# A 512-token attention and ConvFFN layer in split fp32: one plain column pair taken out and the transfers at three seams reordered

## The chip, the cores and the metric

The kernel runs on one NeuronCore of a Trainium2 chip. The metric is device time of one execution in microseconds (us), as the median of the runs shown; less is better. One profiled execution of the kernel before is read beside these runs.

## What is computed

One decoder layer over x (512 tokens, 2048 wide, float32): an attention block and then a feed-forward block, each between two RMS norms and added to its input. The change lies wholly in the second:

```python
h = rms_norm(x, norm_g[i, 2])
x = x + rms_norm(conv_ffn(h, ffn_w_up[i], ffn_conv[i], ffn_w_down[i]), norm_g[i, 3])

def conv_ffn(h, w_up, conv_w, w_down):
    u = h @ w_up                       # 2048 x 11264
    c = causal width-3 depthwise convolution of u over the tokens
    gate, val = jnp.split(c, 2, axis=-1)
    return (jax.nn.silu(gate) * val) @ w_down      # 5632 x 2048
```

## The kernel before

**Numbers.** Every float32 operand is split into a high and a low part (`hi`, `lo`, type fp32r), and a product is three matmuls, high by high, high by low and low by high (`prod`, all recorded at L83). Of each 128 x 1024 weight block (512 KB) ScalarE (ACT) makes the high part at L64 and VectorE (DVE) the low part at L65. The tiles are named `raw` or `bw` (the block as loaded), `wh` and `wl` (its parts), `ah` and `al` (the parts of the normed activations).

**Up-projection.** Its 11264 columns are worked in 44 column pairs f, each 128 gate columns and 128 value columns for all 512 tokens. The two halves of a pair go through `gate` (L583 to L594: convolution, SiLU, product), and GpSimd's queue (POOL) stores the result to `hd` in device memory.

- Pairs 0 and 1 run inside the norm (`up_part`, banks 0, 1, 2 and 5 of PSUM), 256 tokens at a time.
- Pair 2 is `up`: 96 matmuls with 512 columns into banks 3 and 4. Beside it DVE and ACT make the sums of token blocks (`token_sums`, L625 to L632) whose split forms (`settle`, L613 to L617: `f5`, `f6`, `f4` and the kept `k7`, `k1`) all later pairs use. The temporary tiles of that work (`xp`, `xb`, the tile `xf`) are given back behind it (`temps.close()`), and the six buffers `bw` take their place.
- Pair 3 is `up_by_tokens`: the same sums as 192 matmuls with 256 columns, into banks 2 and 5, tokens 0 to 255 ahead of tokens 256 to 511. The parts of `ah` and `al` that are thus done with are overwritten by the last two forms (from `k7` and `k1`).
- Pairs 4 to 43 are `up_pair`: seven products in place of eight, each of 24 matmuls with 256 columns (168 in all). DVE adds blocks first: the first weight form of a pair is the sum of its blocks `b11` and `b21` (L697), the later ones come at L704, L708 and L711; ACT copies results out of PSUM at L688 (`s1`, `s7`, `s2`, `s3`).

**Sums of down weights.** Between the pairs the kernel also makes sums of the down-projection's weights and stores them to `td` in device memory, by `weight_sums` (loads `ts` on SP, adds on DVE at L147, stores at L148) and `queue_sums` (loads on SP, adds and stores by POOL's queue). Six of the 22 groups of these are made in the attention block, the other 16 beside the pairs, two in every five pairs.

**Down-projection.** Seven `product`s, each of 22 steps kp of 12 matmuls with 512 columns. A step needs one weight block `raw` from `td` or from the down weights, and activations `hq` from `hd`, which `fetch` brings in batches of four steps (512 KB).

**What sets the order.** SyncE's queue (SP) issues the loads of `bw`, `ts`, `hq` and, in the down-projection, `raw` in the order of the program (`in_turn`, L139). An issue that must wait, for a free buffer or for data stored earlier, holds back all that stand behind it. DVE, ACT and POOL also run in a fixed order that the scheduler makes from the program. At three places one stage's buffers turn into the next one's, and these are the seams: between pairs 3 and 4, where the pairs with seven products begin; in pairs 40 and 41, where the last sums are made, their space on the right side of SBUF (`tsu`) is given to `hq10` (16 steps of the first activations) and fetched; and between pair 43 and product 0, where `rest`, with `hq10b` (the other six steps), and the second pair of `raw` buffers (`wraw2`) take the place of the up-projection's tiles.

Of the kernel before, what the change touches and what calls it, by code (L numbers as in the profile page):

```python
# [18 lines left out]
P = 128  # L19
# [22 lines left out]
def trunk(ctx, tc, xT, x, grow, table, onehot, masked, sinks, conv,  # L42
# [14 lines left out]
    def bank(i):  # L57
        return ps.tile([P, 512], F32, name=f"b{i}", bufs=1)
# [47 lines left out]
    def project(o, dram, u0):  # L106
        o3 = o.rearrange("p (a b) -> p a b", a=NT)
        for u in range(2):
            w = weights(dram, u0 + u)
            for k in range(8):  # L110
                kt = u * 8 + k
                prod(o3, cols(w, k), moving(kt), kt == 0, kt == KT - 1)
                yield
# [455 lines left out]
    def fetch(m, par, g0, g1):  # L569
        t, k0 = next((t, k) for t, k, k1 in hq[m, par] if k <= g0 < k1)  # L570
        in_turn(t[:, g0 - k0:g1 - k0, :], hd[m, par, :, g0:g1, :])

    with ExitStack() as us:
# [14 lines left out]
        def gate(f, o):  # L588
            cg = conv_half(o[0], f, 0)
            nc.scalar.activation(cg, cg, AF.Silu)  # L590
            cv = conv_half(o[1], f, 1)
            nc.vector.tensor_tensor(cv, cg, cv, ALU.mult)  # L592
            kp, par = divmod(f, 2)
            nc.gpsimd.dma_start(hd[:, par, :, kp, :].rearrange("m p t -> p m t"),  # L594
                              cv.rearrange("p (m t) -> p m t", m=2))
# [37 lines left out]
                if sign:  # L633
                    settle(n, t, k, sign)

        def up(f):
            o = [bank(k) for k in (3, 4)]
            for half in range(2):
                for _ in project(o[half], wup, 4 * f + 2 * half):
                    pass  # L640
            gate(f, o)

        def up_by_tokens(f):
            o = [bank(k) for k in (2, 5)]
            w = {(h, u): weights(wup, 4 * f + 2 * h + u) for h in range(2) for u in range(2)}
            for m in range(2):
                for h in range(2):
                    o3 = o[h].rearrange("p (a b) -> p a b", a=NT)[:, 2 * m:2 * m + 2, :]
                    for kt in range(KT):
                        prod(o3, cols(w[h, kt // 8], kt % 8), moving(kt, 2 * m, 2 * m + 2), kt == 0, kt == KT - 1)  # L650
                n = (7, 1)[m]
                for c in range(2):
                    k = slice(4 * c, 4 * c + 4)
                    settle(n, kept[n][:, :, k, :], k, (-1.0, 1.0)[m])
            gate(f, o)
# [2 lines left out]
        token_sums(0)  # L658
        gate(1, o[2:4])
        token_sums(1)  # L660
        up(2)
        temps.close()
        bw = us.enter_context(pool("bw", 6))
        un = us.enter_context(pool("un", 1))
        up_by_tokens(3)
        held.close()
        tsu = ExitStack()
        sums = tsu.enter_context(pool("tsu", 4, side="right"))
# [22 lines left out]
        def up_pair(f, g):  # L691
            X, Y, Z = (bank(k) for k in ((0, 1, 6), (3, 4, 7))[f % 2])
            ug = un.tile([P, S], F32, name="ug", bufs=2)
            uv = un.tile([P, S], F32, name="uv", bufs=2)
            b11, b21 = block(f, 0, 0), block(f, 1, 0)
            t = wraw.tile([P, 1024], F32, name="raw")
            nc.vector.tensor_tensor(t, b11, b21, ALU.add)  # L697
            times(X, 2, form(t), True)
            s1 = shot(X, "s1")
            step(g)  # L700
            b12 = block(f, 0, 1)
            times(Z, 7, form(b12), True)
            s7 = shot(Z, "s7")
            nc.vector.tensor_tensor(t, t, b12, ALU.add)  # L704
            times(X, 5, form(t), False)
            s2 = shot(X, "s2")
            step(g)
            nc.vector.tensor_tensor(b11, b11, b12, ALU.add)  # L708
            times(Z, 6, form(b11), False)
            b22 = block(f, 1, 1)  # L710
            nc.vector.tensor_tensor(t, t, b22, ALU.add)  # L711
            times(X, 3, form(t), False)
            s3 = shot(X, "s3")
            step(g)
            nc.vector.tensor_tensor(ug[:, :HALF], Z[:, :HALF], s2, ALU.subtract)
            times(Y, 1, form(b21), True)
            nc.vector.tensor_tensor(uv[:, :HALF], s3, s7, ALU.subtract)
            times(X, 4, form(b22), False)
            nc.vector.tensor_tensor(ug[:, HALF:], s1, Y[:, :HALF], ALU.subtract)
            nc.scalar.activation(uv[:, HALF:], X[:, :HALF], AF.Copy, scale=-1.0)  # L720
            gate(f, (ug, uv))

        kp = 6
        for f in range(4, NF):
            i = f - 4
            if i % 5 == 0 and kp < NP:
                work = weight_sums(kp, sums, True)
                step(work)
                kp += 1
            up_pair(f, work if i % 5 == 1 else iter(()))  # L730
            if i % 5 == 1:
                step(work)
            if i % 5 == 1 and kp < NP:
                queue_sums(kp, sums)
                kp += 1
            if kp == NP and tsu:
                tsu.close()
                tsu = None
                early = ctx.enter_context(pool("early", 1, side="right"))
                hq[1, 0] = [(early.tile([P, 16, HALF], F32, name="hq10"), 0, 16)]  # L740
                for g0, g1 in batches[:4]:
                    fetch(1, 0, g0, g1)


    acts.close()
# [3 lines left out]
    y = acc.tile([P, NT, D], F32, name="y")  # L749
    g3 = acc.tile([P, D], F32, name="g3")  # L750
    rest = ctx.enter_context(pool("rest", 1))
    hq[1, 0].append((rest.tile([P, NP - 16, HALF], F32, name="hq10b"), 16, NP))
    raws = (wraw, ctx.enter_context(pool("wraw2", 2)))
    for m, par in ((0, 1), (1, 1)):
        hq[m, par] = [(rest.tile([P, NP, HALF], F32, name=f"hq{m}{par}"), 0, NP)]
    small = ctx.enter_context(pool("small3", 4))
    last = ctx.enter_context(ExitStack())
    hq[0, 0] = [(last.enter_context(pool("hq00", 1)).tile([P, NP, HALF], F32, name="hq00"), 0, NP)]
    coming = [(1, 0, *g) for g in batches[4:]] + [(*q, *g) for q in ((0, 0), (0, 1), (1, 1)) for g in batches]
    nc.scalar.dma_start(g3, grow[2:3, :].to_broadcast([P, D]))  # L760

    XB, ZB = (3, 4, 6, 7), (0, 1, 2, 5)
# [16 lines left out]
        return hi, lo  # L779

    def weight_form(src, kp):
        raw = raws[kp % 2].tile([P, 1024], F32, name="raw")
        table, q = src
        in_turn(raw, td[kp, :, q, :] if table else wdn[4 * kp + q])
        hi, lo = halves()
        split(hi, lo, raw)
        return hi, lo
# [5 lines left out]
    def product(o, form, src, fresh, tail=0):  # L793
        kept = []
        for g0, g1 in batches:
            af = act_form(*form, g0, g1)
            for kp in range(g0, g1):
                wf = weight_form(src, kp)
                if coming and kp % 2 == 0:
                    fetch(*coming.pop(0))  # L800
                if kp >= NP - tail:
                    kept.append((kp, af, g0, wf))
                    continue
                for t in range(2):
                    for e in range(2):
                        multiply(o, kp, af, g0, wf, t, e, fresh)
        return kept
# [135 lines left out]
```

## Time and profile before

| | |
|---|---|
| Median of 3 runs | 1907.91 us (1906.57 to 1908.58) |
| Profiled execution | 1905.1 us, of which the span is 1903.1 us |
| Mean granted TensorE clock | 0.988 of full |
| TensorE (PE) matmul | 1859.6 us, 98% of the span, 11822 instructions |
| DVE, ACT, POOL | 1456.7 us (77%), 982.3 us (52%), 124.0 us (7%) |
| Chain that ended last | PE 62%, issue 2%, DMA 1%, DVE 1% |
| DMA | 392.02 MB, mean 206 GB/s |
| PE waits for `wh` of ACT (L64) | 25.3 us in 4 waits, the longest 16.4 us |
| PE waits for `wl` of DVE (L65), for `s` of ACT (L688) | 4.3 us in 4 waits, 2.6 us in 1 |

In the rows further down, times are us from the start of the span. A row of the timeline gives the start, the duration, the engine, the line, the operation with the tile that it writes and those it reads, and in square brackets how long the engine had stood idle just before and whose work ended that. An engine's name with a q at its end (SPq) is its queue, which issues transfers; the time in such a row is that of issuing. A row of the windows gives for one stretch its length and each engine's busy time with the number of instructions, then the granted TensorE clock (1.00 is full), the share in which the DMA engines were busy, and what they moved.

### The profile page before, as it was taken

To read this page: it belongs to the slowest core of one execution; us is meant where nothing else is said; L and a number is where in the kernel's file an instruction comes from. 1 tells how busy PE (TensorE), PEld (TensorE's weight loads), DVE (VectorE), ACT (ScalarE), POOL (GpSimd) and SP (SyncE) were. 2 spreads that over 40 slices of the span, in tenths; PEclk is the share of its full clock that TensorE was granted. 3 is DMA by queue.
4 is the path that set the end of the run, shared out by engine and by line. 5 is a ranking of instruction groups with operands and counts; after the bars stand their busy time and mean duration, and the time that the engine had idled before them with its cause. 6 is when DMAs were issued, how large, how long until landed. Compare 5 with 4: busy or idle time off the path is not lost.

```text
span 1903.1 us, 30165 instructions
## 1 busy us (share of the span) xinstructions
PE 1859.6 (98%) x11822; PEld 1688.7 (89%) x11822; DVE 1456.7 (77%) x2047; ACT 982.3 (52%) x1566; POOL 124.0 (7%) x196
## 2 busy tenths in 40 slices
PE   9999999999999599999999999999998999999998
PEld 7888888888899599999999999999997888888886
DVE  5468888754787689898989898989875666666875
ACT  6357777622443355555555555555544555545553
POOL 0000000012100111101010101010100000000000
PEclk9999999999999799999999999999998999999999
DMA  9533234499641767667585758575652876575673
GB/s 306 157 98 97 93 119 144 149 348 335 245 166 61 263 190 255 210 228 232 200 249 211 244 202 266 193 242 206 200 208 90 326 275 212 176 245 187 245 249 113
DMA packets 112397, 392.02 MB, mean 206 GB/s; under 512 B 13216, under 2 KB 15488, under 8 KB 110336
## 3 DMA queue, kind: packets, MB, share of 16 engines
q1 hardware_dynamic: 83968, 293.86, 44.8%
q0 software_dynamic: 24256, 87.04, 14.4%
q10 hardware_dynamic: 4032, 9.21, 1.5%
q8 instruction: 92, 1.51, 0.3%
q14 instruction: 49, 0.40, 0.1%
HBM read 309.29 MB, written 72.39 MB: 201 GB/s over the span
## 4 chain that ended last, share of the span: by engine, by line
PE 62%; issue 2%; DMA 1%; DVE 1%; ACT 0%; POOL 0%; DVEq 0%; SPq 0%; ACTq 0%; POOLq 0%
PE b L83 62%; DMA bw<-in_wup 0%; DMA raw<-td 0%; DVE wl L65 0%; DMA hd<-c 0%; DVE x L839 0%; POOL hd L594 0%; DVE raw L697 0%; DVE bw L708 0%; ACT wh L64 0%; ACT junk L828 0%; DVE y L830 0%; DVEq L939 0%; DVE c L592 0%; SPq L139 0%
## 5 line engine op out<-in xcount | busy, mean ns | idle before, releaser
L64 ACT ACTIVATE wh<-raw 128x1024 fp32r<-128x1024 f32 (+1 forms) x371 | 388.9, 1056 | 485.0 <-PE b L83 275.8
L65 DVE TENSOR_TENSOR wl<-raw,wh 128x1024 fp32r<-128x1024 f32 (+1 forms) x371 | 449.6, 1219 | 212.0 <-ACT wh L64 210.6
L83 PE MATMUL b<-ah,wh 128*128 128x256 f32 (+1 forms) x1824 | 563.6, 309 | 18.5 <-ACT wh L64 18.5
L83 PE MATMUL b<-ah,wl 128*128 128x256 f32 (+1 forms) x1824 | 557.2, 305 | 2.6 <-DVE wl L65 2.6
L83 PE MATMUL b<-al,wh 128*128 128x256 f32 (+1 forms) x1824 | 556.3, 305 | 0.4 <-DVE al L65 0.4
L83 PEld LDWEIGHTS b<-ah,wh 128*128 128x128 f32 x1824 | 351.1, 192 | 31.0 <-ACT wh L64 20.4
L83 PEld LDWEIGHTS b<-ah,wl 128*128 128x128 f32 x1824 | 350.6, 192 | 18.3 <-DVE wl L65 3.6
L83 PEld LDWEIGHTS b<-al,wh 128*128 128x128 f32 x1824 | 351.2, 193 | 10.9 <-DVE al L65 0.6
L83 PE MATMUL b<-wh 128*128 128x512 f32 x616 | 241.2, 392 | 6.8 <-ACT wh L64 6.8
L64 ACT ACTIVATE wh<-bw 128x1024 fp32r<-128x1024 f32 x160 | 169.1, 1059 | 147.8 <-PE b L83 144.1
L83 PE MATMUL b<-wl,wh 128*128 128x512 f32 x616 | 241.4, 392 | 1.7 <-DVE wl L65 1.7
L83 PE MATMUL b<-wh,wl 128*128 128x512 f32 x616 | 241.1, 391 | 0.0
L65 DVE TENSOR_TENSOR wl<-bw,wh 128x1024 fp32r<-128x1024 f32 x160 | 194.2, 1218 | 7.6 <-ACT wh L64 6.7
L83 PEld LDWEIGHTS b<-wh 128*128 128x128 f32 x616 | 116.4, 189 | 32.2 <-ACT wh L64 7.8
L83 PEld LDWEIGHTS b<-wl,wh 128*128 128x128 f32 x616 | 116.5, 189 | 26.7 <-DVE wl L65 2.6
L83 PEld LDWEIGHTS b<-wh,wl 128*128 128x128 f32 x616 | 116.5, 189 | 24.1
L83 PE MATMUL b<-wh,ah 128*128 128x512 f32 x320 | 126.5, 395 | 0.0
L83 PE MATMUL b<-wh,al 128*128 128x512 f32 x320 | 124.8, 390 | 0.0
L83 PE MATMUL b<-wl,ah 128*128 128x512 f32 x320 | 124.6, 389 | 0.0
L83 PE MATMUL b<-f6h,wh 128*128 128x256 f32 x320 | 91.4, 286 | 2.6 <-ACT s L688 2.6
L83 PE MATMUL b<-f6l,wh 128*128 128x256 f32 x320 | 91.3, 285 | 0.0
L83 PE MATMUL b<-f6h,wl 128*128 128x256 f32 x320 | 91.2, 285 | 0.0
(165 smaller groups left out, 3031.8 us busy)
## 6 DMA issues: line engine op xcount, KB each, us to landing
bw<-in_wup SPq DMA_DIRECT2D x160, 512.0 KB, 4.4
td<-ts POOLq DMA_DIRECT2D x88, 512.0 KB, 5.4
raw<-td SPq DMA_DIRECT2D x88, 512.0 KB, 5.0
raw<-in_wdn SPq DMA_DIRECT2D x66, 512.0 KB, 4.5
ts<-in_wdn SPq DMA_DIRECT2D x64, 512.0 KB, 6.2
ts<-in_wdn POOLq DMA_DIRECT2D x40, 512.0 KB, 8.4
raw<-in_wq SPq DMA_DIRECT2D x32, 512.0 KB, 3.5
raw<-in_wo SPq DMA_DIRECT2D x32, 512.0 KB, 5.0
```

Source lines behind the costliest of these rows:

```text
L64: nc.scalar.activation(hi, src, AF.Copy)
L65: nc.vector.tensor_tensor(lo, src, hi.bitcast(F32), ALU.subtract)
L83: tc.keep_in_program_order(nc.tensor.matmul(o, l, r, start=start, stop=stop, skip_group_check=more))
```

## The change

It takes `up` and its call for pair 2 out: `up_by_tokens` now makes pair 2, and the pairs with seven products begin at f=3, so there are 41 of them in place of 40. The first `weight_sums` beside the pairs moves from before the first such pair (i=0) to before the second (i=1), with its adds in the third (i=2). The early fetch of `hq10` moves out of pair 40 to after the loop and is cut from four batches to two, so that `hq10b` now holds 14 steps. `wraw2` is opened on the right side beside the smaller `hq10`, and the `raw` buffers are taken in turn from `wraw`, `wraw`, `wraw2`, `wraw2`, in place of one pool for even and one for odd kp. In product 0 the fetches come at the weight forms of kp 3, 4, 5 and 6, then at even kp from 8.

```diff
--- before.py
+++ after.py
@@ -633,13 +633,6 @@
                 if sign:
                     settle(n, t, k, sign)
 
-        def up(f):
-            o = [bank(k) for k in (3, 4)]
-            for half in range(2):
-                for _ in project(o[half], wup, 4 * f + 2 * half):
-                    pass
-            gate(f, o)
-
         def up_by_tokens(f):
             o = [bank(k) for k in (2, 5)]
             w = {(h, u): weights(wup, 4 * f + 2 * h + u) for h in range(2) for u in range(2)}
@@ -658,11 +651,10 @@
         token_sums(0)
         gate(1, o[2:4])
         token_sums(1)
-        up(2)
         temps.close()
         bw = us.enter_context(pool("bw", 6))
         un = us.enter_context(pool("un", 1))
-        up_by_tokens(3)
+        up_by_tokens(2)
         held.close()
         tsu = ExitStack()
         sums = tsu.enter_context(pool("tsu", 4, side="right"))
@@ -721,25 +713,26 @@
             gate(f, (ug, uv))
 
         kp = 6
-        for f in range(4, NF):
-            i = f - 4
-            if i % 5 == 0 and kp < NP:
+        for f in range(3, NF):
+            i = f - 3
+            if (i == 1 or i and i % 5 == 0) and kp < NP:
                 work = weight_sums(kp, sums, True)
                 step(work)
                 kp += 1
-            up_pair(f, work if i % 5 == 1 else iter(()))
-            if i % 5 == 1:
+            adding = i == 2 or i > 5 and i % 5 == 1
+            up_pair(f, work if adding else iter(()))
+            if adding:
                 step(work)
-            if i % 5 == 1 and kp < NP:
-                queue_sums(kp, sums)
-                kp += 1
-            if kp == NP and tsu:
-                tsu.close()
-                tsu = None
-                early = ctx.enter_context(pool("early", 1, side="right"))
-                hq[1, 0] = [(early.tile([P, 16, HALF], F32, name="hq10"), 0, 16)]
-                for g0, g1 in batches[:4]:
-                    fetch(1, 0, g0, g1)
+                if kp < NP:
+                    queue_sums(kp, sums)
+                    kp += 1
+        assert kp == NP
+        tsu.close()
+        early = ctx.enter_context(pool("early", 1, side="right"))
+        hq[1, 0] = [(early.tile([P, 8, HALF], F32, name="hq10"), 0, 8)]
+        wraw2 = ctx.enter_context(pool("wraw2", 2, side="right"))
+        for g0, g1 in batches[:2]:
+            fetch(1, 0, g0, g1)
 
 
     acts.close()
@@ -749,14 +742,14 @@
     y = acc.tile([P, NT, D], F32, name="y")
     g3 = acc.tile([P, D], F32, name="g3")
     rest = ctx.enter_context(pool("rest", 1))
-    hq[1, 0].append((rest.tile([P, NP - 16, HALF], F32, name="hq10b"), 16, NP))
-    raws = (wraw, ctx.enter_context(pool("wraw2", 2)))
+    hq[1, 0].append((rest.tile([P, NP - 8, HALF], F32, name="hq10b"), 8, NP))
+    raws = {"pools": (wraw, wraw, wraw2, wraw2), "next": 0}
     for m, par in ((0, 1), (1, 1)):
         hq[m, par] = [(rest.tile([P, NP, HALF], F32, name=f"hq{m}{par}"), 0, NP)]
     small = ctx.enter_context(pool("small3", 4))
     last = ctx.enter_context(ExitStack())
     hq[0, 0] = [(last.enter_context(pool("hq00", 1)).tile([P, NP, HALF], F32, name="hq00"), 0, NP)]
-    coming = [(1, 0, *g) for g in batches[4:]] + [(*q, *g) for q in ((0, 0), (0, 1), (1, 1)) for g in batches]
+    coming = [(1, 0, *g) for g in batches[2:]] + [(*q, *g) for q in ((0, 0), (0, 1), (1, 1)) for g in batches]
     nc.scalar.dma_start(g3, grow[2:3, :].to_broadcast([P, D]))
 
     XB, ZB = (3, 4, 6, 7), (0, 1, 2, 5)
@@ -779,7 +772,8 @@
         return hi, lo
 
     def weight_form(src, kp):
-        raw = raws[kp % 2].tile([P, 1024], F32, name="raw")
+        raw = raws["pools"][raws["next"] % 4].tile([P, 1024], F32, name="raw")
+        raws["next"] += 1
         table, q = src
         in_turn(raw, td[kp, :, q, :] if table else wdn[4 * kp + q])
         hi, lo = halves()
@@ -796,7 +790,7 @@
             af = act_form(*form, g0, g1)
             for kp in range(g0, g1):
                 wf = weight_form(src, kp)
-                if coming and kp % 2 == 0:
+                if 3 <= raws["next"] - 1 <= 6 or coming and kp % 2 == 0 and raws["next"] > 7:
                     fetch(*coming.pop(0))
                 if kp >= NP - tail:
                     kept.append((kp, af, g0, wf))
```

Three places, as the order of instructions shows them. SP's queue at the first seam, as a piece of the difference; `raw<-in_wup` are the weight blocks of pairs 2 and 3, `bw` the blocks of the pairs with seven products, four for each, and `ts` the down weights to be added:

```order
-L77 DMA raw<-in_wup 128x1024 x11
+L77 DMA raw<-in_wup 128x1024 x7
+L139 DMA bw<-in_wup 128x1024 x4
+L139 DMA ts<-in_wdn 128x1024 x4
+L139 DMA bw<-in_wup 128x1024 x8
+L139 DMA ts<-in_wdn 128x1024 x4
+L139 DMA bw<-in_wup 128x1024 x8
 L139 DMA ts<-in_wdn 128x1024 x4
```

Four `raw` loads are gone, and the first pair's four blocks now stand ahead of the first four `ts` loads, behind them before.

DVE at the end of `up_by_tokens`, in the kernel before (the number behind a name tells tiles of one name apart; `b2` and `b5` are the PSUM banks, `c0` and `c1` the gate's tiles, `raw` the first sum of blocks):

```order
L615 SCALAR_TENSOR_TENSOR f4l_5458<-xf_5519,f4h_5457 128x2x512
L592 TENSOR_TENSOR c1_5652<-c0_5647,c1_5652 128x512
L615 SCALAR_TENSOR_TENSOR al_76<-k7_5459,ah_75 128x2x512 x2
L584 SCALAR_TENSOR_TENSOR c0_5892<-b2_5666,cw_83,c0_5892 128x511
L585 SCALAR_TENSOR_TENSOR c0_5892<-b2_5666,cw_83,c0_5892 128x510
L617 TENSOR_TENSOR al_76<-k1_5460,ah_75 128x2x512 x2
L584 SCALAR_TENSOR_TENSOR c1_5897<-b5_5667,cw_83,c1_5897 128x511
L585 SCALAR_TENSOR_TENSOR c1_5897<-b5_5667,cw_83,c1_5897 128x510
L592 TENSOR_TENSOR c1_5897<-c0_5892,c1_5897 128x512
L147 TENSOR_TENSOR ts_5909<-ts_5909,ts_5907 128x1024
L147 TENSOR_TENSOR ts_5907<-ts_5907,ts_5908 128x1024
L147 TENSOR_TENSOR ts_5908<-ts_5908,ts_5909 128x1024
L147 TENSOR_TENSOR ts_5910<-ts_5910,ts_5908 128x1024
L697 TENSOR_TENSOR raw_5924<-bw_5920,bw_5922 128x1024
```

and in the changed kernel, from the read of bank 5 that gate(1) makes (line numbers behind the removed function are lower by 6 to 8, so L689 is L697 before):

```order
L585 SCALAR_TENSOR_TENSOR c1_5501<-b5_4997,cw_83,c1_5501 128x510
...
L615 SCALAR_TENSOR_TENSOR f4l_5458<-xf_5519,f4h_5457 128x2x512
L584 SCALAR_TENSOR_TENSOR c0_5759<-b2_5533,cw_83,c0_5759 128x511
L585 SCALAR_TENSOR_TENSOR c0_5759<-b2_5533,cw_83,c0_5759 128x510
L617 TENSOR_TENSOR al_76<-k1_5460,ah_75 128x2x512 x2
L584 SCALAR_TENSOR_TENSOR c1_5764<-b5_5534,cw_83,c1_5764 128x511
L585 SCALAR_TENSOR_TENSOR c1_5764<-b5_5534,cw_83,c1_5764 128x510
L592 TENSOR_TENSOR c1_5764<-c0_5759,c1_5764 128x512
L689 TENSOR_TENSOR raw_5783<-bw_5779,bw_5781 128x1024
```

The four adds at L147 no longer stand between the gate's last product (L592) and the first sum of blocks, and `up_by_tokens` writes banks 2 and 5 directly behind pairs 0 and 1, of which pair 1 used the same two banks.

SP's queue at the second and third seams, as a piece of the difference (`hq_14936` and `hq_15751` are `hq10` in the two kernels; the `bw` rows are pairs 39 to 43, the `raw` rows product 0):

```order
-L139 DMA bw<-in_wup 128x1024 x12
-L139 DMA ts<-in_wdn 128x1024 x4
-L139 DMA bw<-in_wup 128x1024 x8
-L139 DMA ts<-in_wdn 128x1024 x4
-L139 DMA hq_14936<-hd 128x1024 x4
-L139 DMA bw<-in_wup 128x1024 x12
+L139 DMA bw<-in_wup 128x1024 x6
+L139 DMA hq_15751<-hd 128x1024 x2
+L139 DMA bw<-in_wup 128x1024 x10
+L139 DMA raw<-td 128x1024 x4
+L139 DMA hq10b<-hd 128x1024
 L139 DMA raw<-td 128x1024
 L139 DMA hq10b<-hd 128x1024
-L139 DMA raw<-td 128x1024 x2
+L139 DMA raw<-td 128x1024
```

Before, the fetch of `hq10` stands directly behind the last `ts` loads and ahead of 12 blocks; now six blocks stand between them. Before, one `raw` load stands ahead of the first `hq10b`; now four do.

## Rows read from the trace of the kernel before

**Rows 1.** The page's first part: busy us, share of the span, instructions of each engine.

```profile
PE 1859.6 (98%) x11822; PEld 1688.7 (89%) x11822; DVE 1456.7 (77%) x2047; ACT 982.3 (52%) x1566; POOL 124.0 (7%) x196
```

**Rows 2.** Timeline of PE: six of its idle stretches at the three seams.

```profile
640.58 0.58 PE L83 MATMUL b<-ah,wh 128*128 128x256 f32 x1 [16.39 <-ACT wh L64]
...
655.88 0.38 PE L83 MATMUL b<-f6h,wh 128*128 128x256 f32 x1 [2.62 <-ACT s L688]
...
1397.03 0.53 PE L83 MATMUL b<-ah,wh 128*128 128x256 f32 x1 [2.12 <-ACT wh L64]
...
1464.58 0.50 PE L83 MATMUL b<-wh 128*128 128x512 f32 x1 [2.97 <-ACT wh L64]
...
1466.35 0.79 PE L83 MATMUL b<-wl,wh 128*128 128x512 f32 x1 [1.27 <-DVE wl L65]
...
1475.27 0.79 PE L83 MATMUL b<-wh 128*128 128x512 f32 x1 [3.86 <-ACT wh L64]
```

**Rows 3.** Windows: pairs 2, 3, 4, 5, 40, 41 and products 0, 1.

```profile
579.21:601.00 21.79, 21.79 (x99) 18.02 (x98) 20.82 (x20) 10.46 (x12) 1.47 (x2) 1.00 0.23 73
601.00:624.19 23.19, 23.19 (x193) 22.98 (x191) 7.49 (x9) 6.13 (x7) 0.71 (x1) 1.00 0.04 13
640.58:668.99 28.41, 23.98 (x168) 23.43 (x169) 22.25 (x22) 12.06 (x15) 3.19 (x4) 0.84 0.89 301
668.99:689.15 20.16, 20.16 (x170) 20.16 (x169) 17.34 (x20) 10.75 (x15) 3.28 (x5) 1.00 0.89 275
1374.59:1397.03 22.44, 20.32 (x171) 20.12 (x169) 10.11 (x13) 7.12 (x12) 2.66 (x4) 1.00 0.86 304
1397.03:1421.13 24.10, 23.33 (x169) 22.88 (x170) 22.09 (x25) 13.41 (x19) 0.74 (x1) 0.86 0.40 128
1464.58:1534.72 70.14, 64.55 (x264) 52.03 (x265) 41.52 (x36) 33.13 (x34) 0.71 (x1) 0.90 0.87 318
1534.72:1594.56 59.84, 59.84 (x265) 49.55 (x264) 40.39 (x36) 30.57 (x33) 0.00 (x0) 1.00 0.65 228
```

**Rows 4.** Windows: three stretches at half clock.

```profile
656.40:659.80 3.40, 3.40 (x18) 3.40 (x18) 3.06 (x3) 0.65 (x2) 1.77 (x2) 0.50 1.06 396
1397.10:1403.90 6.80, 6.03 (x27) 5.74 (x28) 6.80 (x9) 2.69 (x5) 0.00 (x0) 0.50 0.34 118
1465.40:1479.00 13.60, 8.33 (x18) 5.75 (x19) 3.89 (x4) 3.58 (x4) 0.71 (x1) 0.50 0.78 277
```

**Rows 5.** Timeline of DVE beside pairs 2 and 3.

```profile
586.78 0.74 DVE L585 SCALAR_TENSOR_TENSOR c<-b,cw,c 128x510 f32<-128x510 f32 x1
...
603.37 1.22 DVE L615 SCALAR_TENSOR_TENSOR f4l<-xf,f4h 128x1024 fp32r<-128x1024 f32 x1
```

**Rows 6.** Timeline of DVE between pairs 3 and 4.

```profile
628.01 0.69 DVE L592 TENSOR_TENSOR c<-c,c 128x512 f32<-128x512 f32 x1
631.60 1.22 DVE L147 TENSOR_TENSOR ts<-ts 128x1024 f32<-128x1024 f32 x1 [2.89 <-DMA ts<-in_wdn]
...
638.22 1.22 DVE L697 TENSOR_TENSOR raw<-bw 128x1024 f32<-128x1024 f32 x1 [1.36 <-DMA bw<-in_wup]
```

**Rows 7.** Timeline of SP's queue between pairs 3 and 4.

```profile
626.56 1.75 SPq L139 DMA_DIRECT2D ts<-in_wdn  x4
628.36 3.49 SPq L139 DMA_DIRECT2D bw<-in_wup  x6
```

**Rows 8.** Timeline of SP's queue from pair 39 to pair 40.

```profile
1354.46 2.22 SPq L139 DMA_DIRECT2D ts<-in_wdn  x4
1383.63 2.60 SPq L139 DMA_DIRECT2D hq<-hd  x4
```

**Rows 9.** Timeline of SP's queue from pair 42 to product 0.

```profile
1428.59 0.33 SPq L139 DMA_DIRECT2D raw<-td  x1
1468.25 0.33 SPq L139 DMA_DIRECT2D hq10b<-hd  x1
1468.80 0.79 SPq L139 DMA_DIRECT2D raw<-td  x2
```

**Rows 10.** Timeline of ACT in product 0.

```profile
1474.16 2.20 ACT L64 ACTIVATE wh<-raw 128x1024 fp32r<-128x1024 f32 x2 [9.63 <-DMA raw<-td]
```

## Prediction

> **What bounds the kernel now.** The page's first part comes first: PE's matmuls fill 98% of the span [rows 1], so only matmul time, PE's idle stretches and stretches in which its clock is down can be gained. The timeline of PE, searched for idle rows, then shows where it stands: at the three seams [rows 2]. The reader is to see there how long each wait is and that each ends with a weight form (`wh`, `wl`) or with a copy out of PSUM (`s`). Third, the windows give each stage's price. The undisturbed measures are 20.16 us for a pair with seven products and 59.84 us for a product; disturbed are pair 4 (28.41), pairs 40 and 41 (22.44 and 24.10) and product 0 (70.14) [rows 3]. Part of that is no idling: behind the waits the granted clock is 0.50, the lower of its two levels, 1.2 GHz [rows 4]. Last, the timelines of DVE and SP's queue say why the form that ended each wait was late [rows 5 to 10].
>
> The sum is made against the profiled execution, 1905.1 us; the median of the runs shown is 1907.9, which is 2.8 more, and I add that at the end. About 0.2% (3.8 us) is what a measurement here can tell from no change.
>
> **A plain pair becomes a seven-product pair.** Pair 2 takes 21.79 us for 96 matmuls with 512 columns, 227 ns each; an undisturbed pair takes 20.16 us for 168 with 256, 120 ns each [rows 3]. The swap is worth 21.79 - 20.16 = 1.6 us; it is inside the sum of the first seam below. The Trainium skill speaks against it (TensorE: Matmul & The Clock Gate, Back-to-back issue gap): sustained spacing of about 81 ns at 128 columns and 131 ns at 512. An estimate from these, some 98 ns at 256, makes the plain pair 12.6 us and the seven products 16.4, so the swap would cost 3.8 and the sum below would be 5.4 smaller. The rows contradict that, and the measurement decides: 512 columns cost nearly twice what 256 do, so fewer columns in all are less time.
>
> **First seam, from 579.21 to the start of pair 5.** Before: 21.79 + 23.19 + 16.39 of idling + 28.41 = 89.78 us [rows 2, 3]. After, the same stretch holds pair 2 by tokens, the gap, pair 3 with seven products and pair 4:
>
> - *Pair 2 by tokens*: 23.19 [rows 3], plus a new wait. It writes banks 2 and 5, and pair 1's gate still reads them; before, pair 2 on banks 3 and 4 stood between. Its second quarter, on bank 5, would begin at 579.21 + 23.19/4 = 585.0, but DVE reads bank 5 until 586.78 + 0.74 = 587.5 [rows 5]: 2.5 us of idling. Behind a wait of 2.62 the clock was down for 3.40 us, which costs half, 1.7; behind 2.12 for 6.80, which costs at most 3.4 [rows 2, 4]. I take 2.4.
> - *Gap*: DVE ends the gate's last product at 628.70, 4.5 us after pair 3's end at 624.19, whatever follows [rows 3, 6]. Before, that product is followed by four adds that wait for `ts` loads issued at 626.56, and by the first sum of blocks, whose `bw` loads stand behind these on SP [rows 6, 7]. After, SP's `bw` loads come first. They need the buffers of the temporaries, whose last reader is `f4l` at 603.37 [rows 5]; without pair 2's weight forms, three of some 1.2 us ahead of it, DVE reaches it about 4 us earlier. A load takes 5.0 us from issue to use (626.56 to 631.60) [rows 6, 7], so the blocks are there well ahead of the end of pair 2 by tokens, about 607. Then sum of blocks, split and matmul take 640.58 - 638.22 = 2.4 [rows 2, 6]. Gap: 4.5 + 2.4 = 6.9.
> - *Pair 3*: 20.16 plus what pair 4 suffers now. Pair 4's 8.25 over is 4.43 of idling (28.41 less 23.98 busy) and 3.8 of clock [rows 3]. The clock's part stays; of the idling, the copy `s7`, which stands in ACT's order behind weight forms, still comes late: I take 1.2 of the 2.62 [rows 2]. That is 25.2; its bounds are 24.0 (no idling) and 28.4 (all of it).
> - *Pair 4*: 20.16. The `ts` loads now stand ahead of its blocks on SP and their adds among DVE's; pair 5, with 0.89 of DMA and 17.34 us of DVE, carries such work at full pace [rows 3]. Were that cover gone, its first sum would wait one load, 5.0.
>
> Sum: 23.19 + 2.5 + 2.4 + 6.9 + 25.2 + 20.16 = 80.4, a gain of 9.4 us. With the bounds, 78.5 to 84.6: a gain of 5.2 to 11.3.
>
> **Second seam.** SP issues the last `ts` loads at 1354.46 and then stands before the fetch of `hq10` until 1383.63, because it needs the space that the last stores of `td` read from; pair 41's blocks wait behind it and are issued only at 1386.2 [rows 8]. PE waits 2.12 at 1397.03, and the clock falls [rows 2, 4]: pairs 40 and 41 together take 46.54 against 40.32, 6.2 lost [rows 3]. After, the last `ts` loads come a pair earlier and six blocks stand ahead of the fetch, one and a half pairs of PE's work; only two batches follow instead of four. The stores, done some 29 us after the `ts` loads, have then gone by or nearly so when SP comes to the fetch. Gain 6.2; if a wait remains that costs as much as the first one did, 4.1.
>
> **Third seam.** Product 0 takes 70.14 against 59.84, 10.3 over [rows 3]: 64.55 of busy time make 4.7 of clock, the other 5.6 is idling, of which 1.27 at its start and 3.86 at 1475.27 [rows 2]. Ahead of it lie another 2.97 in pair 43. The 2.97 and the 1.27 come from DVE and ACT, which work through the last gate; their order is the same after, so both stay. The 3.86 is a `raw` that came late: SP had issued one at 1428.59, then stood before `hq10b`, which needs space of the last gate, until 1468.25 and could issue the next two only at 1468.80 [rows 9]; ACT stood 9.63 for them [rows 10]. After, four `raw` loads stand ahead, enough for four steps of 2.72 (59.84/22), about 11 us, and the fifth is issued some 7 us after pair 43's end and lands 5.0 later, in time. What remains is 1.27 and clock: 1.7 at least, 4.7 at most [rows 3, 4]; I take 2.9, since PE no longer stops a third time. That makes 4.2 over in place of 10.3: a gain of 6.1, between 4.3 and 7.3.
>
> **Edits that cost nothing.** `wraw2`'s earlier opening and the rotation of the buffers move no instruction of PE. The fetches move in number from neither product: eleven stand in each of products 0 and 1, and only four of them come closer together at kp 3 to 6. Product 0 covers these with its DMA at 0.87 [rows 3]; if that is not enough, the fourth rival applies. The end of the program is the same work.
>
> Sum of the gains: 9.4 + 6.2 + 6.1 = 21.7; 1905.1 - 21.7 = 1883.4 profiled, and with 2.8 the median is **1886 us**. All bounds at their low end give 13.6, so 1894; all at their high end 24.8, so 1883.
>
> **Rivals.**
>
> - *First: blocks late at the first seam* (chance 0.14). The space for `bw` comes free only with the last settle, at 626.5, 2.3 after the end of the by-tokens pair. The sum of blocks then follows a load of 5.0 to 9.9 (628.36 to 638.22) [rows 6, 7], so the gap is 2.3 + 7.4 + 2.4 = 12.1, 5.2 more, and pair 3 suffers about 1.5 more: **1893 us**. For it: the pool takes the place of several tiles at once. Against it: the order has the loads waiting for `f4l` alone.
> - *Second: the fetch still holds SP* (0.08). Its two transfers stand among pair 41's blocks, not behind the loop's end as the text of the program says. If stores and space come free as late as before, the 6.2 stays: **1892 us**. Against it: 29 us of standing before [rows 8] is spent on a pair and a half of other blocks now.
> - *Third: lighter first seam* (0.07). DVE drops the work of pair 2's weight forms and reads bank 5 before PE wants it; the 2.5 and 2.4 fall away: **1881 us**. Against it: DVE is the same in that stretch but for these, and it was 20.82 of 21.79 busy [rows 3].
> - *Fourth, on the other side: the products become bound by loads* (0.06). A step needs one weight block and half a fetch, 786 KB in 2.72 us, 289 GB/s, and four fetches now crowd into kp 3 to 6, 1.05 MB a step. Where DMA falls behind, each step waits for its `raw`. Nothing is lost down to 289 GB/s; to undo the gain and reach 0.2% over, 25.5 us over 44 steps, a step must take 3.30 us, which is 238 GB/s. At 230 GB/s it is 3.42 a step, 31 us in all: **1917 us**. For it: product 0 had DMA at 0.87 [rows 3]. Against it: the same product moved 318 GB/s, and product 1 ran without a stop [rows 3]. The Trainium skill (DMA: Bandwidth & Descriptors, Issuing engines are not separate DMA queues) has all transfers run on the same 16 engines and interleave, so no reordering makes them faster; that agrees with the 0.87 here, and no row shows the engines at their limit in the products.
>
> **How the numbers follow.** The forecast has 0.65, with 1883 to 1894 as its own range. The range takes in the first three rivals, the third at 1881 with 1 us to spare: **1880 to 1895**. Out of it lies the fourth, with the tail of two rivals together. Faster by over 0.2%, below 1904: 0.65 + 0.14 + 0.08 + 0.07 = **0.94**. Of the fourth's 0.06, 0.02 is a light case that only eats the gain (**same, 0.02**) and **0.04** is slower.
>
> **What would show it.** Right: PE's first seven-product matmul about 7 us behind the end of pair 2 by tokens, a wait of 2.5 in that pair's second quarter, released by DVE at L585, and pair 3 near 25; no idle row and no half clock at pairs 40 and 41, all of them 20.2; product 0 near 64 us with no wait on `raw<-td`. The first seam's size is the least certain of the three terms: a gap of 12 there would mean the first rival, a gain below 4 at the third that the clock and not the `raw` was its price. Wrong: SP's row of `hq<-hd` long behind its neighbours beside late `bw` blocks, idle rows through products 0 and 1 that end with DMA, or a plain time that stays within 4 us of before.

## The result and the profile after

The changed kernel takes 1881.55 us (median of 4 runs, 1880.45 to 1882.65) against 1907.55 before: a ratio of 0.986, 95% interval 0.985 to 0.988. The profiled execution took 1881.34 us, its span is 1879.1; the profiled one before took 1905.1. The two differ by 23.8 us. The forecast was 1886 (1880 to 1895), with 1883 to 1894 as its own range without the rivals.

PE's idle rows at the seams, from the timeline of the changed kernel; they answer to [rows 2]:

```profile
588.05 0.36 PE L83 MATMUL b<-ah,wh 128*128 128x256 f32 x1 [2.53 <-DVE c L585]
...
612.35 0.58 PE L83 MATMUL b<-ah,wh 128*128 128x256 f32 x1 [6.80 <-ACT wh L64]
...
624.93 0.39 PE L83 MATMUL b<-f6h,wh 128*128 128x256 f32 x1 [1.00 <-ACT s L680]
...
945.27 0.39 PE L83 MATMUL b<-f5h,wh 128*128 128x256 f32 x1 [0.41 <-ACT s L680]
...
1447.91 0.49 PE L83 MATMUL b<-wh 128*128 128x512 f32 x1 [2.97 <-ACT wh L64]
...
1449.68 0.50 PE L83 MATMUL b<-wl,wh 128*128 128x512 f32 x1 [1.28 <-DVE wl L65]
```

The 16.39 of the first seam is 6.80 and the 2.62 for `s` is 1.00; nothing is left at pairs 40 and 41 of the 2.12; the 3.86 for a `raw` is gone; the 2.97 and the 1.27 stand as they were. New are the 2.53, released by DVE's read of bank 5, and the 0.41.

The windows of the changed kernel: pair 2, the gap, pairs 3 and 4, 19 and 20, 40 and 41, 43, product 0; they answer to [rows 3]:

```profile
579.21:605.55 26.34, 23.81 (x197) 23.43 (x195) 20.86 (x20) 11.02 (x12) 0.73 (x1) 1.00 0.22 75
605.55:612.35 6.80, 0.00 (x1) 0.00 (x0) 6.49 (x7) 2.74 (x4) 0.71 (x1) 0.87 0.73 261
612.35:636.54 24.19, 22.67 (x168) 22.18 (x169) 23.92 (x24) 11.79 (x15) 2.21 (x4) 0.90 0.79 290
636.54:656.70 20.16, 20.16 (x170) 20.16 (x169) 17.27 (x20) 10.02 (x14) 4.53 (x6) 1.00 0.90 287
938.94:959.77 20.83, 20.42 (x170) 20.22 (x169) 17.84 (x20) 10.40 (x15) 3.21 (x5) 1.00 0.84 255
959.77:980.53 20.76, 20.41 (x170) 20.21 (x169) 18.77 (x22) 10.68 (x16) 0.73 (x1) 1.00 0.35 114
1363.57:1384.30 20.73, 20.41 (x171) 20.21 (x169) 17.58 (x21) 10.40 (x15) 0.73 (x1) 1.00 0.47 164
1384.30:1404.46 20.16, 20.16 (x171) 20.16 (x169) 17.04 (x20) 10.63 (x15) 0.72 (x1) 1.00 0.35 117
1424.62:1447.91 23.29, 20.32 (x171) 20.12 (x169) 13.34 (x18) 11.36 (x18) 0.71 (x1) 1.00 0.35 126
1447.91:1511.02 63.11, 61.83 (x264) 50.82 (x265) 41.13 (x36) 32.74 (x34) 0.72 (x1) 0.97 0.89 330
```

Where the time went, stretch by stretch: from 579.21 to the start of pair 5, 89.78 before and 656.70 - 579.21 = 77.49 after, 12.3 less (0.4 of the 77.49 was there before the pair: PE's last idle row ahead of it stands at 560.91, before at 560.52); pairs 40 and 41, 46.54 and 40.89, 5.7 less; product 0, 70.14 and 63.11, 7.0 less. Pairs 19 and 20 give 1.3 back. Together 23.7 of the 23.8.

The gap of 6.80 is made as forecast: on DVE the first sum of blocks (L689) now follows the last product of the gate (L592) at once, and that product still ends 4.5 us behind pair 2:

```profile
609.38 0.69 DVE L592 TENSOR_TENSOR c<-c,c 128x512 f32<-128x512 f32 x1
609.99 1.22 DVE L689 TENSOR_TENSOR raw<-bw 128x1024 f32<-128x1024 f32 x1
```

SP's queue of the changed kernel, at the three seams; it answers to [rows 7], [rows 8] and [rows 9]:

```profile
599.97 2.86 SPq L139 DMA_DIRECT2D bw<-in_wup  x4
607.93 1.75 SPq L139 DMA_DIRECT2D ts<-in_wdn  x4
...
1323.28 2.00 SPq L139 DMA_DIRECT2D ts<-in_wdn  x4
1330.74 23.01 SPq L139 DMA_DIRECT2D bw<-in_wup  x6
1360.52 0.80 SPq L139 DMA_DIRECT2D hq<-hd  x2
...
1409.56 19.06 SPq L139 DMA_DIRECT2D raw<-td  x4
1451.73 0.32 SPq L139 DMA_DIRECT2D hq10b<-hd  x1
```

The first pair's blocks are issued at 599.97, 5.6 us before pair 2 ends; the fetch of `hq10` still stands from 1353.75 to 1360.52, but 37 us behind the last `ts`, with six blocks gone ahead; and four `raw` loads are out 23 us or more before `hq10b` gets its space at 1451.73.

### The profile page after: what moved, and what is told of

Same layout as the page of the kernel before. It is cut to its first block, busy times and chain, and to the rows that moved or that the text cites. A ratio compares the mean times of both kernels' runs of the same rounds, so it can differ in the third digit from the quotient of the medians.

```text
span 1879.1 us, 30357 instructions
## 1 busy us (share of the span) xinstructions
PE 1851.6 (99%) x11894; PEld 1685.4 (90%) x11894; DVE 1463.6 (78%) x2057; ACT 986.1 (52%) x1574; POOL 123.9 (7%) x196
## 4 chain that ended last, share of the span: by engine, by line
PE 61%; DVE 2%; DMA 2%; issue 1%; ACT 1%; DVEq 0%; ACTq 0%
PE b L83 61%; DMA bw<-in_wup 2%; DVE wl L65 1%; ACT wh L64 0%; DVE c L585 0%; DVE c L584 0%; DVE raw L703 0%; DVE bw L700 0%; DVE x L833 0%; ACT s L680 0%; DVE ug L711 0%; ACT c L583 0%; ACT junk L822 0%; DVE y L824 0%; ACT uv L712 0%
## 5 line engine op out<-in xcount | busy, mean ns | idle before, releaser
L64 ACT ACTIVATE wh<-bw 128x1024 fp32r<-128x1024 f32 x164 | 173.2, 1058 | 144.4 <-PE b L83 142.2
L65 DVE TENSOR_TENSOR wl<-bw,wh 128x1024 fp32r<-128x1024 f32 x164 | 199.2, 1218 | 4.8 <-ACT wh L64 4.4
L83 PE MATMUL b<-f5h,wh 128*128 128x256 f32 x328 | 92.9, 283 | 0.4 <-ACT s L680 0.4
L83 PE MATMUL b<-f5l,wh 128*128 128x256 f32 x328 | 92.8, 283 | 0.0
```

The lines of the kernel that those rows point to most:

```text
L64: nc.scalar.activation(hi, src, AF.Copy)
L65: nc.vector.tensor_tensor(lo, src, hi.bitcast(F32), ALU.subtract)
L83: tc.keep_in_program_order(nc.tensor.matmul(o, l, r, start=start, stop=stop, skip_group_check=more))
```

## The experiments

The kernel before took 1906.7, 1906.7 and 1906.5 us in the three sets of runs, against 1907.55 beside the changed kernel, which was not run again in them; so up to some 1 us of a difference can lie between the sets. Differences are between medians, against the changed kernel's 1881.55 where no other kernel is named.

**One seam put back at a time.** First seam:

```diff
-            if (i == 1 or i and i % 5 == 0) and kp < NP:
+            if i % 5 == 0 and kp < NP:
-            adding = i == 2 or i > 5 and i % 5 == 1
+            adding = i % 5 == 1
```

> The changed kernel with the first seam's order alone put back: the first loads of ts stand ahead of the first seven-product pair's blocks again (i = 0), the adds come in the second pair. My theory (the order on SP's queue and DVE makes the first seam's gain): the idling between pair 2 by tokens and pair 3 goes from 6.85 back to about 16 us, and pair 3 from 24.2 to about 28, so 13 to 14 us more than the changed kernel, some 1895 us. Rival (the gain at this seam comes from the plain pair that was taken out): the gap stays under 9 us, and the time within 3 us of the changed kernel's 1881.6.

1892.64 us, 11.1 more. The idle row of PE ahead of pair 3, in the timeline of this run:

```profile
624.11 0.58 PE L83 MATMUL b<-ah,wh 128*128 128x256 f32 x1 [17.32 <-ACT wh L64]
```

The gap is back in full, with the plain pair still gone; pair 3 took 25.1 here, not 28. So the order makes this gain, and the rival falls. The edit puts back both the order on SP's queue and the adds on DVE; DVE's rows of this run part the two:

```profile
610.62 0.69 DVE L592 TENSOR_TENSOR c<-c,c 128x512 f32<-128x512 f32 x1
614.20 1.22 DVE L147 TENSOR_TENSOR ts<-ts 128x1024 f32<-128x1024 f32 x1 [2.89 <-DMA ts<-in_wdn]
616.51 3.75 DVE L147 TENSOR_TENSOR ts<-ts 128x1024 f32<-128x1024 f32 x3 [1.08 <-DMA ts<-in_wdn]
621.74 1.23 DVE L689 TENSOR_TENSOR raw<-bw 128x1024 f32<-128x1024 f32 x1 [1.49 <-DMA bw<-in_wup]
```

Of the 10.4 us between the gate's last product and the first sum of blocks, 5.5 is waiting for loads and 5.0 the four adds. The other 3.3 us of pair 4's 28.41 [rows 3] do not come back with it.

Second seam, the fetch alone, moved into the loop behind the last sums:

```diff
+            if kp == NP and tsu:
+                tsu.close()
+                tsu = None
...
+                for g0, g1 in batches[:2]:
+                    fetch(1, 0, g0, g1)
```

> The changed kernel with the fetch of hq10 put back directly behind the last sums, ahead of the next pairs' blocks on SP's queue; two batches, as in the change. My theory (the place in the queue counts): SP stands before the fetch for some 29 us, the two pairs behind it lose about 6 us to a wait and a lower clock; some 1887.5 us. Rival (the size counts, two batches in place of four): under 2 us lost, 1882 to 1883 us.

1885.39 us, 3.8 more: between the two. SP stood 25.7 us before the fetch here, from the last `ts` on, against 6.8 in the changed kernel:

```profile
1323.12 1.94 SPq L139 DMA_DIRECT2D ts<-in_wdn  x4
1350.80 0.82 SPq L139 DMA_DIRECT2D hq<-hd  x2
```

What it waits for is the last store of `td`. POOL issues that store later in the changed kernel (first row) than here (second row):

```profile
1353.44 0.54 POOL L160 DMA_DIRECT2D td<-ts  x1 [5.26 <-DMA ts<-ts]
```

```profile
1347.34 0.54 POOL L160 DMA_DIRECT2D td<-ts  x1 [3.58 <-DMA ts<-ts]
```

With six blocks loading beside them there, the last four stores took 7.3 us from issue to landing (median), and 5.0 here. So the blocks put ahead of the fetch also delay what the fetch waits for. The same with four batches:

```diff
-                hq[1, 0] = [(early.tile([P, 8, HALF], F32, name="hq10"), 0, 8)]
-                for g0, g1 in batches[:2]:
+                hq[1, 0] = [(early.tile([P, 16, HALF], F32, name="hq10"), 0, 16)]
+                for g0, g1 in batches[:4]:
```

> As the kernel with the fetch put back directly behind the last sums, but with four batches in place of two (hq10 of 16 steps; the second pair of raw buffers then has to open on the left, as before the change, so that product 0 waits again and only the pairs are to be compared). Pairs 39 and 40 lost 3.5 us with two batches there; before the change the pairs behind the fetch lost 6.2. Theory (the place and the size both count): with four batches they lose 6 us or more. Rival (the place alone counts, the rest of the 6.2 lies elsewhere): 3.5 us again.

The windows of pairs 39 and 40, of the run with two batches and then of that with four:

```profile
1343.70:1366.99 23.29, 21.52 (x169) 21.32 (x168) 14.80 (x17) 9.43 (x14) 1.33 (x3) 0.94 0.79 270
1366.99:1387.52 20.53, 20.53 (x171) 20.53 (x171) 19.40 (x22) 11.67 (x18) 0.73 (x1) 0.99 0.39 131
```

```profile
1343.30:1364.11 20.81, 20.40 (x171) 20.20 (x169) 9.95 (x13) 7.03 (x12) 1.93 (x4) 1.00 0.89 312
1364.11:1387.67 23.56, 20.96 (x168) 20.35 (x169) 22.04 (x25) 13.42 (x20) 0.73 (x1) 1.00 0.43 140
```

Two batches cost 43.82 - 40.32 = 3.5 us, four 44.37 - 40.32 = 4.1 (its 1893.07 us holds the third seam's wait as well). With four, PE idles 3.0 in four waits and the clock stays at 1.00; before the change it idled 2.9 at the same place, but then ran at 0.50 for a stretch [rows 3, 4]. So four batches add 1.2 us of idling (3.0, against 23.29 - 21.52 = 1.8 with two) but only 0.6 in all: my theory's 6 us do not come, and the rival's 3.5 is nearer. The rest of the 6.2 is the clock, which fell behind some of these waits and not behind others.

Third seam, the `raw` buffers and the fetches' places as before the change:

```diff
-    raws = {"pools": (wraw, wraw, wraw2, wraw2), "next": 0}
+    raws = (wraw, ctx.enter_context(pool("wraw2", 2)))
-                if 3 <= raws["next"] - 1 <= 6 or coming and kp % 2 == 0 and raws["next"] > 7:
+                if coming and kp % 2 == 0:
```

> The changed kernel with the third seam put back: wraw2 opened behind rest on the left side, raw buffers by even and odd kp, fetches at even kp from 0, so that one raw load stands ahead of the first hq10b in place of four. My theory: PE waits near 4 us for a raw again, product 0 goes from 63.1 to about 70 us, some 1888.5 us. Rival (the gain at this seam is only the lower clock behind the waits, which does not hang on the raw loads): product 0 under 65 us, within 2 us of 1881.6.

1890.16 us, 8.6 more. The windows of product 0 and its idle row:

```profile
1447.59:1518.97 71.38, 66.10 (x264) 53.03 (x265) 41.44 (x36) 33.26 (x34) 0.72 (x1) 0.90 0.85 315
```

```profile
1458.10 0.79 PE L83 MATMUL b<-wh 128*128 128x512 f32 x1 [3.69 <-ACT wh L64]
```

The wait returns, and with it 66.10 - 61.83 = 4.3 us of slower matmuls. The rival falls.

**The plain pair kept**, all seams as changed (`up(2)` ahead of `up_by_tokens(3)`, the pairs from 4):

> The changed kernel with the plain pair 2 kept ahead of the pair by tokens (which makes pair 3), all three seams as in the change. My theory: the plain pair costs 21.8 against 20.2 us (1.6 more), and the 2.5 us wait for bank 5 goes, since banks 3 and 4 stand between again: about 1 us less than the changed kernel, 1880.5 us, not to be told from it. First rival (the skipped pair carries the first seam's gain): over 5 us more, 1887 us or above. Second rival (by the Trainium skill's sustained spacing the plain pair is the cheaper one): some 6 us less, 1875 us.

1878.53 us: 3.0 *less* than the changed kernel. None of the three fits in size. The sign is my theory's and the second rival's; the rival's reason falls, as the plain pair is the dearer one here too, 21.79 us against 20.16. Its windows, the plain pair, the pair by tokens, the gap and the first seven-product pair:

```profile
579.21:601.00 21.79, 21.79 (x99) 18.03 (x98) 20.79 (x20) 10.47 (x12) 1.47 (x2) 1.00 0.23 73
601.00:624.16 23.16, 23.16 (x193) 22.95 (x191) 7.50 (x9) 6.13 (x7) 0.71 (x1) 1.00 0.29 103
624.16:630.96 6.80, 0.00 (x1) 0.01 (x1) 6.49 (x7) 2.75 (x4) 0.72 (x1) 0.82 0.48 170
630.96:653.65 22.69, 22.18 (x169) 21.89 (x169) 22.46 (x23) 10.59 (x14) 2.18 (x4) 0.90 0.78 288
```

Pair 5 begins at 653.65, in the changed kernel at 656.70. The swap's 1.6 us are there, but the 2.5 for bank 5 and 1.5 in the first seven-product pair take them back. Of that 1.5, 1.0 is the wait for the copy `s`, which is missing here; beside it DVE has 23.92 us of work in the pair against 22.46 (why it has more was not looked into). Most of the other 0.6 was there before the pair (PE's idle row at 560.91 against 560.49). Pairs 19 and 20 show no wait here. So taking the pair out, by itself, makes this kernel 2 to 3 us slower, and the reordered seams carry the whole gain.

**The wait for the bank**, by another pair of banks:

```diff
-            o = [bank(k) for k in (2, 5)]
+            o = [bank(k) for k in (0, 1)]
```

> The changed kernel with pair 2 by tokens on banks 0 and 1 (which pair 0's gate has given back by then) in place of 2 and 5. My theory (the skipped plain pair had hidden a wait for bank 5, which makes the swap a loss of 3 us in place of a gain of 1.6): the wait of 2.53 us in pair 2 goes, and with it a short stretch at half clock that some executions show there: 2.5 to 4 us less than the changed kernel, some 1878.5 us, level with the kernel that keeps the plain pair. Rival (the wait only moves, since DVE has the same work to do before the end of the pair): the gap ahead of pair 3 grows from 6.8 to about 9.3, and the time stays at 1881.5 us.

1877.47 us, 4.1 less. Its window of pair 2 has no idling left, and the gap behind it grows by 0.5 alone:

```profile
579.21:602.37 23.16, 23.16 (x194) 22.96 (x192) 20.50 (x20) 10.93 (x12) 0.73 (x1) 1.00 0.05 16
602.37:609.70 7.33, 0.00 (x1) 0.00 (x0) 5.94 (x7) 2.81 (x5) 0.71 (x1) 0.74 0.87 302
```

The wait was the bank, and two numbers remove it; the rival, by which it would only move, falls. The swap then stands level with the plain pair. Pair 5 begins 2.8 us earlier; the rest is pairs 19 and 20, undisturbed here.

**What is left of the third seam.** Product 0's first forms ahead of the last gate, kept in the program's order on ACT and DVE (pinned), with the first bank of product 0 exchanged; the run does not part the two:

```diff
+            if f == NF - 1:
+                first_forms()
...
-            gate(f, (ug, uv))
+            gate(f, (ug, uv), f == NF - 1)
...
-    XB, ZB = (3, 4, 6, 7), (0, 1, 2, 5)
+    XB, ZB = (6, 4, 3, 7), (0, 1, 2, 5)
```

> The changed kernel with the activation form and the first two weight forms of product 0 made ahead of pair 43's last gate on ACT and DVE (pinned in that order), and product 0's first bank swapped with its third, since the gate reads bank 3 last. My theory (the 2.97 and 1.28 us of waits at the third seam and 2 us of lower clock behind them are the order on ACT and DVE, not a transfer): both waits go, product 0 near 60 us and pair 43 near 20.2, 5 to 6 us less than the changed kernel, some 1876 us. Rival (the transfers of raw or the space for the new tiles set this wait): PE still waits 2 us or more there, 1880 us or above.

1882.56 us: nothing gained. Pair 43 is 20.16 and the 2.97 and 1.28 are gone, but the timelines of PE and of SP's queue show a new wait, four steps later:

```profile
1461.18 0.50 PE L83 MATMUL b<-wh 128*128 128x512 f32 x1 [3.06 <-ACT wh L64]
```

```profile
1454.33 0.32 SPq L139 DMA_DIRECT2D hq10b<-hd  x1
1454.70 0.42 SPq L139 DMA_DIRECT2D raw<-td  x1
```

PE came to the fifth step earlier, and the fifth `raw` still stood behind `hq10b`. So the rival's time came, and by a late `raw`; whether its transfer or its place in the queue made it late, the next run shows. With the fetches two weight forms later:

```diff
-                if 3 <= raws["next"] - 1 <= 6 or coming and kp % 2 == 0 and raws["next"] > 7:
+                if 5 <= raws["next"] - 1 <= 8 or coming and kp % 2 == 0 and raws["next"] > 9:
```

> As the kernel with the activation form and two weight forms of product 0 made early (1882.6 us, where the two waits at the seam went, 3.1 us of pair 43 with them, and a wait of 3.06 us for raw at kp 5 came in their place), with the four hq10b fetches two weight forms later, so that six raw loads stand ahead of the first of them on SP. My theory (the new wait is SP standing before hq10b, which needs the last gate's space, as at this seam before the change): the 3.06 goes, product 0 some 61 us with pair 43 at 20.2, so 5 us less than the changed kernel, 1876.5 us. Rival (the transfers' rate at the start of product 0 sets the pace, six raws and four fetches at once): a wait of 2 us or more comes again one or two steps later, 1880 us or above.

1874.78 us, 6.8 less, pair 43 and product 0 in the windows:

```profile
1426.27:1446.43 20.16, 20.16 (x171) 20.16 (x169) 12.75 (x15) 10.02 (x14) 0.71 (x1) 1.00 0.45 145
1446.43:1507.03 60.60, 60.16 (x267) 49.48 (x265) 41.56 (x39) 33.62 (x37) 0.72 (x1) 1.00 0.88 331
```

Both steps of my theory hold: PE's longest wait in product 0 is 0.43, so at 331 GB/s the transfers' rate does not bind.

**What is left of the first seam**, on the kernel with the plain pair. The first pair's block sums and first three weight forms are traced, and pinned, ahead of the by-tokens pair's last settle:

```diff
+                if m:
+                    open_pair(f + 1, True)
                 n = (7, 1)[m]
```

The first try of it pinned the first sum of every pair behind all that DVE had been given before:

> The kernel that keeps the plain pair (1878.5 us), with the first three weight forms of the first seven-product pair made ahead of the last settle and gate of the pair by tokens. My theory (what is left of the first seam's gap is the order on DVE and ACT: the first sum of blocks stands behind the settle and the gate though its blocks came long before): the gap of 6.8 us goes, pair 4 near 20.5 in place of 22.7; some 9 us less, 1869.5 us. First rival (DVE's work is only moved into pair 4, which then waits for DVE): half comes back, 1874 us. Second rival, which adds to either: the fetch of hq10 now stands two blocks behind the last sums in place of six, and costs some 2 us at pairs 40 to 41.

2173.08 us, a fault of the edit. Pair 4 itself began without a gap, but from then on PE stood for `wh` 32 times, 192.4 us in all, most often at the start of a pair, as here at pair 6:

```profile
679.20 0.58 PE L83 MATMUL b<-ah,wh 128*128 128x256 f32 x1 [6.12 <-ACT wh L64]
```

Pinned for the first pair alone:

> As the run before it that made three weight forms of the first seven-product pair ahead of the last settle and gate, but with the order pinned for that first pair alone (in the earlier kernel the first sum of every pair was pinned behind the gate before it, which cost each pair 6 us). In that earlier run the first pair itself began without a gap and took some 20.3 us. My theory (the first seam's gap is the order on DVE and ACT, no transfer): against the kernel that keeps the plain pair (1878.5 us) the gap of 6.8 us goes and pair 4 takes some 20.3 us in place of 22.7: 9 us less, 1869.5 us. Rival (DVE's work is only moved into pairs 4 and 5, which then wait for DVE): half comes back, 1874 us.

1871.50 us, 7.0 less than the kernel with the plain pair. Windows of pairs 4 and 5:

```profile
623.72:643.88 20.16, 20.16 (x171) 20.16 (x169) 17.10 (x19) 8.59 (x13) 2.89 (x5) 1.00 0.82 313
643.88:666.66 22.78, 20.93 (x171) 20.31 (x169) 21.59 (x25) 12.18 (x18) 2.54 (x3) 1.00 0.74 263
```

The gap goes and pair 4 is undisturbed; pair 5, with DVE 21.59 of 22.78 busy, gives 2.6 us back. That is the rival's mechanism at a part of its price. SP's loads at this seam stand in the same order in both runs, so what was left of the gap was the order on DVE and ACT. Both edits on the kernel with the plain pair:

> The plain pair kept, with both edits: the first seven-product pair's forms ahead of the last settle, and product 0's first forms ahead of the last gate with the hq10b fetches two steps later. If the two seams are independent, the sum of the two: 9 us from the first, 5 from the third, off 1878.5: some 1864.5 us. If only the first seam's edit holds: 1869.5; if only the third's: 1873.5.

1865.71 us (ratio to before 0.979, 0.977 to 0.980): 5.8 below the first seam's edit alone. The seams nearly add up, and this kernel beats the kernels with one of the edits.

## Why the prediction was right

The mechanism is the forecast one: the three seams carry the gain, as put back one by one: 11.1, 3.8 and 8.6 us. The number owes something to luck. 1881.55 is inside the stated 1880 to 1895 but below the forecast's own 1883 to 1894. The range reached down to it only for the third rival at 1881, whose reason did not come about: it wanted no wait for bank 5, and the 2.53 is there. Term by term, forecast and measured:

- *The whole*: 1883.4 profiled, measured 1881.3. The 2.8 added for the median did not come back: the profiled execution after lies 0.2 below its median. That makes over half of the 4.5 us by which 1886 was too high.
- *First seam*: 9.4, measured 12.3, above the 11.3 that was its upper bound. The gap was worked out at 6.9 and is 6.80; the wait for bank 5 at 2.5 and is 2.53. The step that was mis-sized is the clock: I took 2.4 behind the 2.53, and the profiled execution kept its full clock there; pair 3 is 24.19, not 25.2, as clock cost 2.5 and not 3.8. The 2.4 was too high in any case: the same 2.53 was followed by half clock in five of the seven traces that have it, and from that wait to the end of pair 2 these took 18.9 to 19.0 us, against 17.5 in the two at full clock, so it cost 1.4 to 1.5 or nothing. The first and third rivals did not come about: no late blocks, and the bank does bind.
- *Second seam*: 6.2, measured 5.7. The place of the fetch is worth 3.8 of it. That the stores would "have gone by or nearly so" was the weak step: SP still stood 6.8 us before the fetch, as the blocks put ahead slowed the stores themselves, and pair 40 lost 0.6. The second rival so holds in its mechanism and not in its price.
- *Third seam*: 6.1, measured 7.0; the clock behind the 1.28 cost 2.0, not 2.9.
- *The swap*: the text named 1.6 as its worth. Its own terms, 2.5 and 2.4 in pair 2 less 1.6, already made it a loss of 3.3, which I summed into the seam and never said; kept alone, the plain pair is 3.0 faster. The Trainium skill's sustained spacings (TensorE: Matmul & The Clock Gate, Back-to-back issue gap) have the sign of that result but not its cause: the plain pair is 21.79 us against 20.16 in the run that keeps it, so the rows stay against them.
- *Not foreseen*: 1.3 us in pairs 19 and 20, where ACT's copies of `s` came late. The same pairs lost over 0.5 us in three of the seven traces with pair 2 on banks 2 and 5 (the changed kernel and both with product 0's early forms). What sets them off was not tried and stays open.
- *Fourth rival, loads in the products*: products 1 to 5 took 59.84 each, as before; it does not hold. That the fetches "move in number from neither product" was a miscount: products 0 and 1 together bring 22 in place of 20, the two that the early fetch gave up. It cost nothing. The aside that no reordering makes transfers faster does not hold for a single one: the stores of `td` took 7.3 or 5.0 us by the order alone.

## What to carry to other kernels

Where a stage's first transfer needs space that the stage before gives back last, put everything that is already free to load ahead of it on its queue; how many loads stand ahead then decides how long the stop is covered. Price a piece of work that is taken out by what it covered as well as by its own time: here 1.6 us of saving uncovered 2.5 us of a bank still being read, and another bank number was the cure. A wait removed ahead of a queue that is still blocked comes back a few steps later, so follow the next load before counting the gain.

## What was not expected of the hardware

The clock does not answer to a wait of one length in one way. Behind the same 2.53 us wait of PE the stretch from 589.2 was at half clock in the run with the early fetch and at full clock in the changed kernel (windows; the first line is the run with the early fetch):

```profile
589.20:592.60 3.40, 3.40 (x19) 3.40 (x18) 3.40 (x5) 2.65 (x3) 0.64 (x1) 0.50 0.00 0
```

```profile
589.20:592.60 3.40, 3.40 (x31) 3.40 (x30) 3.40 (x4) 2.39 (x3) 0.24 (x1) 1.00 0.00 0
```

19 matmuls against 31 in the same time. So in this kernel a term for the clock behind a wait of 2 to 3 us is a chance and not a fixed price: nothing behind this 2.53, and 3.2 behind the 2.12 of pair 41 before (23.33 busy less 20.16 [rows 3]), where a wait of 0.77 followed it.
